# A two-layer RWKV-7 and attention trunk: the norm factor moved into the inverse blocks, and recurrence steps moved between ScalarE, VectorE and GpSimd

## The chip, the cores and the metric

One core of one Trainium2 chip runs the whole program in one launch. The metric is the device time in microseconds. The engines are PE (TensorE), DVE (VectorE), ACT (ScalarE), POOL (GpSimd) and SP (SyncE, which here only issues DMA transfers; POOL and ACT issue some too).

## The reference

The input x has 1024 tokens of 1024 features in float32. Layer 0 is RWKV-7 time mixing and an MLP, layer 1 forgetting attention and an MLP. The change lies in the time mixing, whose core is, for each of 16 heads of 64 features:

```python
kk = kk / jnp.maximum(jnp.linalg.norm(kk, axis=-1, keepdims=True), 1e-12)
k = k * (1.0 + (a - 1.0) * k_a)
b_h = kk * a_h
def step(S, inp):
    r_t, w_t, k_t, v_t, kk_t, b_t = inp
    sa = jnp.einsum('bhvk,bhk->bhv', S, -kk_t)
    S = (S * w_t[:, :, None, :] + sa[..., None] * b_t[:, :, None, :]
         + v_t[..., None] * k_t[:, :, None, :])
    y_t = jnp.einsum('bhvk,bhk->bhv', S, r_t)
    return S, y_t
...
y = (y - mean) * lax.rsqrt(var + GN_EPS)
y = y * lnx_w + lnx_b
y = (y + bonus) * g
return y @ w_o
```

Before it stand the projections to r, k, v and the low-rank branches for the decay w, for a and for the gate g; after it the residual, and `square(relu(h @ w_in)) @ w_out`.

## The kernel before

The step by step recurrence is computed in 16 chunks of 64 tokens. Within a chunk the tokens' mutual effect is a triangular system, whose inverse is made ahead in blocks of 32 tokens (32x32), for all heads and chunks.

In order of time: the low-rank branches (to about 53 us); the k projection, whose results `prep_pair` turns, pair of heads by pair of heads (8 pairs), into decayed k, kk and b (written to DRAM as `d_KR`, `d_BK`), the blocks `d_N`, and the factor `nt`, one over the squared norm of kk for each token and head (to 203); the r projection (to 281), with the first half of the inverse (`prep_inverse`, b=0) on DVE beside it; the v projection (to 371), with the second half (b=1); the gate projections (`gp`, to about 404); the recurrence, some 15 us a chunk (to about 676); the rest of the trunk.

`prep_inverse` keeps 128 blocks of 32x32 in `Tb` for each of two halves g, solves them with 31 pairs of DVE steps, and writes them to `d_B` and, transposed by a DVE copy into `Nb`, to `d_T`. From there `rec_load_blocks` reads three tiles for a chunk: `B11` and `BT2` (for the corner that joins two blocks of 32) and `TT` (the whole 64x64 inverse, whose off-diagonal corner `rec_corner2` writes). Before, `nt` was not in the blocks but in a table `ns2`, and was multiplied into `B11` and into the solution `Z` of each chunk.

PE's order within chunk c: `pp` (Z by AE, the state's part), an early part of the output `yp` (KR by Z); then `ap` of chunk c+1 (b, k against kk, r), which DVE masks into `AE`; `sa` (the inverse `TT` by `Ps`, the copy of pp), which becomes half of `Z`; `tp` (transposes of b, k, copied to `BKt`); `u` (the new state, needs Z and BKt), the rest of `yp`, the corner products `op`. In chunks 3 and later 24 matmuls of the output projection `wo` are spread over a chunk. KR (kk and r with their decays; its tile and BK's are named KRz in the profile) lies in two buffers, one per parity of chunks. After `ap` of a chunk has read KR, r's half is scaled by the decay of the chunk before (`rec_corner`), for the next early output.

The matrix `w_o` is loaded in 8 parts (`woraw`), each split into a rounded high part on ACT (`woh`) and a low part `wol`. The table WO gives for each part the hook numbers at which its load, its high part and, if a third number is there, its low part on DVE are placed; without the third number the low part is a GpSimd step. ACT's casts `woh` are pinned: `keep_in_program_order` holds them in the order in which they are written among other pinned ACT steps. All other steps are ordered on each engine by a list scheduler with a timeline model; `high_priority(offset=900)` lifts the solve and the state.

The parts on which the prediction's steps rest are the loads in `rec_load`, the end of `rec_corner`, the end of `rec_solve`, and in `stage_recurrence` where the next chunk's loads are asked for:

```python
            prev, cur, Z = cur, nxt, Zn
            if c + 2 < NCH:
                nxt, Zn = load(c + 2)
```

Of the kernel before, what the change touches and what calls it, by code (L numbers as in the profile page):

```python
# [8 lines left out]
F32 = mybir.dt.float32  # L9
# [7 lines left out]
P = 128  # L17
# [12 lines left out]


XAT = (2, 4, 6, 8, 10, 12, 13, 14)
WO = {1: (0, 1), 2: (0, 3), 3: (3, 5), 0: (5, 11), 4: (9, 16, 21), 7: (12, 23, 28), 5: (14, 17), 6: (18, 24)}
# [124 lines left out]
def rwkv_keep(k):  # L158

    cp, dr = k.const, k.dram  # L160

    k.sc = cp.tile([P, NK, NCH], F32, name="sc")
    k.ns2 = cp.tile([P, NK, NCH], F32, name="ns2")

    k.bon = cp.tile([P, NK, H], F32, name="bon")
    k.d_vb = dr.tile([2, T, NK, N], F32, name="d_vb")
    k.d_vh = dr.tile([2, T, NK, N], F32, name="d_vh")
    k.d_KR = dr.tile([NCH, P, NK, 2, C], F32, name="d_KR")
    k.d_BK = dr.tile([NCH, P, NK, 2, C], F32, name="d_BK")
# [33 lines left out]
def head_sums(k, xs, pool):  # L203
# [10 lines left out]
    for j in range(2):  # L214
        nc.tensor.transpose(bank[:, 256 + P * j:256 + P * j + P], rows[:, P * j:P * j + P], k.ident)
# [54 lines left out]
def prep_pair(k, p, units):  # L270

    nc, w = k.nc, k.pw
    nt = w.tile([P, HC, 2], F32, tag="nt", name="nt")
    nc.vector.tensor_scalar(nt.rearrange("p (g j) h -> p g j h", j=2), head_sums(k, [u[0] for u in units], w), 1e-24, -1.0,
                            op0=ALU.max, op1=ALU.mult)
    nc.vector.reciprocal(nt, nt)
    np_ = [k.psA.tile([P, HC, C], F32, tag="psA", name="np_") for _ in HALF]
    for c in range(NCH):
        for h, hs in enumerate(HALF):
            _, KK, BK = units[c // HC]  # L280
            nc.tensor.matmul(np_[h][HALF[c % 2], c // 2], BK[hs, c % HC, 0], KK[hs, c % HC], start=True, stop=True)
    for h in range(2):
        N_ = units[h][1]
        nc.vector.tensor_tensor(N_, np_[h], nt[:, :, h:h + 1].broadcast_to([P, HC, C]), op=ALU.mult)
        u = 2 * (p % 4) + h
        for c in range(2):
            for d in range(2):
                s0 = u % 4 * 32 + (c * 2 + d) * HC
                q = 64 * c + 32 * d
                nc.sync.dma_start(k.d_N[p // 4][u // 4, s0:s0 + HC].rearrange("c i t -> i c t"),  # L290
                                  N_[q:q + 32, :, 32 * d:32 * d + 32])
# [26 lines left out]
def prep_inverse(k, b, pool):  # L318

    nc = k.nc  # L320
    Nb, Tb = (k.pi.tile([P, 2, 32, 32], F32, tag=n, name=n) for n in ("Nb", "Tb"))
    Tm = pool.tile([P, 512], F32, tag="v", name="Tm", bufs=3)
    nc.gpsimd.dma_start(Nb, k.d_N[b].rearrange("g s i t -> s g i t"))
    ones = Tb.rearrange("p g t m -> p g (t m)")
    nc.gpsimd.memset(ones, 0.0)
    nc.gpsimd.memset(ones[:, :, 0:1024:33], 1.0)
    for j in range(31):
        n, m = 31 - j, j + 1
        S = [P, 2, n, m]
# [70 lines left out]
    return Z  # L400


def rec_load(k, c):

    nc, w = k.nc, k.rw
    (KR, BK), TT = k.KRB[c % 2], k.TT[c % 2]
    B11 = k.rc.tile([P, NK, 32], F32, tag="B11", name="B11")
    BT2 = k.rc.tile([P, NK // 2, 32], F32, tag="BT2", name="BT2")
    nc.sync.dma_start(KR, k.d_KR[c])
    nc.sync.dma_start(BK, k.d_BK[c])  # L410
    AE = w.tile([P, NK, 2, 2, C], F32, tag="AE", name="AE")
    BKt = w.tile([P, NK, P], F32, tag="BKt", name="BKt")
    return dict(c=c, KR=KR, TT=TT, BK=BK, B11=B11, BT2=BT2, AE=AE, BKt=BKt)


def rec_load_blocks(k, s):

    nc, c, TT, B11, BT2 = k.nc, *(s[n] for n in ("c", "TT", "B11", "BT2"))
    dT = k.d_T.rearrange("(p r) m t -> r m p t", r=64)
    dB = k.d_B.rearrange("(p r) t m -> r t p m", r=64)  # L420
    r0, r1 = ([32 * h + (2 * (c % 2) + d) * HC + c // 2 for h in range(2)] for d in range(2))
    for h in range(2):
        nc.sync.dma_start(B11[QUART[h]], dB[r0[h]])
# [29 lines left out]
def rec_corner(k, s):  # L453

    nc, c = k.nc, s["c"]
    AE, KR = s["AE"], s["KR"]
    O1 = s["O1"] = k.rw1.tile([P, NK // 2, 32], F32, tag="O1", name="O1")
    op = k.psA.tile([P, NK // 2, 32], F32, tag="psA", name="op")
    for p in range(NK):
        for h, q in enumerate(QUART):  # L460
            k.pe.matmul(op[LANES[h][p % 2], p // 2], AE[q, p, h, 0, 32:64], s["B11"][q, p], start=True, stop=True)
    nc.scalar.copy(O1, op)
    if c:

# [17 lines left out]
def rec_solve(k, s, Z):  # L482

    nc, c = k.nc, s["c"]
    pp = k.psC.tile([P, NK, C], F32, tag="psC", name="pp")
    for p in range(NK):
        for h, hs in enumerate(HALF):
            k.pe.matmul(pp[hs, p], s["AE"][:, p, h, 0, :], Z[:, h, p], start=True, stop=True)
    Ps = k.rw.tile([P, NK, C], F32, tag="Ps", name="Ps")
    if c:  # L490
        nc.scalar.copy(Ps, pp)
    else:
        nc.vector.tensor_copy(Ps, pp)
    yp = s["yp"] = k.psY.tile([P, NK, C], F32, tag="psY", name="yp")
    if c:
        for p in range(NK):
            for h, hs in enumerate(HALF):
                k.pe.matmul(yp[hs, p], s["KR"][hs, p, 1, :], Z[hs, h, p], start=p == 0, stop=False)
    yield
    sa = k.psC.tile([P, NK, C], F32, tag="psC", name="sa")  # L500
    for p in range(NK):
        for h, hs in enumerate(HALF):
            k.pe.matmul(sa[hs, p], s["TT"][:, p, h, :], Ps[:, p], start=True, stop=True)
    for h, hs in enumerate(HALF):
        nc.vector.tensor_tensor(Z[hs, h], sa[hs], k.ns2[hs, :, c:c + 1].broadcast_to([64, NK, C]), op=ALU.mult)
# [30 lines left out]
def rec_norm(k, s):  # L536
# [21 lines left out]
    eng.tensor_tensor(Y, Y, V, op=ALU.add)  # L558
# [1728 lines left out]
```

## Time and profile before

| | |
|---|---|
| median of 3 runs (lowest, highest) | 2512.4 us (2508.08, 2515.24) |
| the profiled execution, its span | 2515.11 us, 2513.4 us |
| mean granted clock of PE | 0.995 |
| busy: PE, DVE, ACT, POOL | 2471.0, 1820.6, 1288.0, 457.0 us |
| HBM | 166 GB/s over the span |

Times in the trace are microseconds from the span's start. A timeline row gives start, length, engine, line, operation, the written tile <- the read ones, shapes, and in brackets the idle time before it with what ended it. A row of waits gives a waiting engine's operation, the releasing one, and the sum, number and longest of the waits. A window of the trace gives each engine's busy time in it, then PE's granted clock, the share of the DMA engines and GB/s.

### The profile page before, as it was taken

The page shows a single profiled execution, that of the slowest core. Times are in us where ns is not written, and L with a number is a line of the kernel's source. Part 1 is how long each engine was busy: PE and PEld are TensorE (multiplying, and loading weights), DVE is VectorE, ACT ScalarE, POOL GpSimd, SP SyncE. Part 2 cuts the span into 40 slices and gives each one's busy share as a digit, 9 for nine tenths or more (in the row PEclk, how much of TensorE's full clock was granted, in tenths as well). Part 3 has the DMA queues.
Part 4 walks back from the last instruction along what each step waited for, and adds up shares of the span by engine and source line. Part 5 has one row for each costly group of instructions (what it writes and reads, how often), then busy time and mean ns, then how long its engine had stood idle before and what let it go on. Part 6 is the DMA issues. An engine that isn't in the chain of part 4 may idle for free.

```text
span 2513.4 us, 43433 instructions
## 1 busy us (share of the span) xinstructions
PE 2471.0 (98%) x16945; PEld 2062.8 (82%) x16945; DVE 1820.6 (72%) x2861; ACT 1288.0 (51%) x2236; POOL 457.0 (18%) x397
## 2 busy tenths in 40 slices
PE   8999998899999999999999999999999999999999
PEld 5777787788888888888889999888888888878887
DVE  7787995888687777477669576888528777656765
ACT  6782464333554555344456453788526455443332
POOL 2221135555200000003002223355100000000210
PEclk9999999999999999999999999999999999999999
DMA  4779668666244454766631325565323545386663
GB/s 140 168 159 225 176 221 221 182 178 172 78 161 150 150 169 167 264 247 238 220 113 51 118 76 169 146 151 144 130 82 120 169 150 171 117 287 236 224 209 135
DMA packets 378801, 419.79 MB, mean 167 GB/s; under 512 B 141786, under 2 KB 257970, under 8 KB 378596
## 3 DMA queue, kind: packets, MB, share of 16 engines
q1 hardware_dynamic: 366196, 389.88, 51.5%
q0 software_dynamic: 5744, 18.69, 2.0%
q10 hardware_dynamic: 6656, 8.46, 1.0%
q8 instruction: 133, 2.18, 0.4%
q14 instruction: 72, 0.59, 0.1%
HBM read 293.02 MB, written 123.92 MB: 166 GB/s over the span
## 4 chain that ended last, share of the span: by engine, by line
PE 90%; DVE 3%; issue 2%; DMA 2%; ACT 2%; POOL 1%; SPq 1%; ACTq 0%; DVEq 0%; POOLq 0%
PE mm L381 42%; PE mm L800 7%; PE mm L801 7%; PE mm L799 7%; PE mm L869 5%; PE tp L384 4%; PE wo L381 3%; PE mm L898 3%; PE s L381 2%; PE o L381 2%; PE z1p L381 1%; PE yp L381 1%; PE ap L381 1%; PE u L381 1%; PE sa L381 1%
## 5 line engine op out<-in xcount | busy, mean ns | idle before, releaser
L381 PE MATMUL mm<-ol,oh 128*128 128x512 f32 x896 | 346.8, 389 | 1.0 <-DVE ol L1614 1.0
L381 PE MATMUL mm<-oh 128*128 128x512 f32 x896 | 346.9, 389 | 0.4 <-ACT oh L1612 0.4
L381 PE MATMUL mm<-oh,ol 128*128 128x512 f32 x896 | 346.6, 389 | 0.0
L763 ACT CAST oh<-ra 128x1024 fp32r<-128x1024 f32 x108 | 113.8, 1054 | 333.3 <-PE mm L381 239.3
L766 DVE TENSOR_TENSOR ol<-ra,oh 128x1024 fp32r<-128x1024 f32 x108 | 137.8, 1276 | 146.9 <-ACT oh L763 146.8
L381 PEld LDWEIGHTS mm<-ol,oh 128*128 128x128 f32 x896 | 168.2, 188 | 36.1 <-DVE ol L1614 1.4
L381 PEld LDWEIGHTS mm<-oh 128*128 128x128 f32 x896 | 168.2, 188 | 35.6 <-ACT oh L1612 0.8
L381 PEld LDWEIGHTS mm<-oh,ol 128*128 128x128 f32 x896 | 168.2, 188 | 35.0
L799 PE MATMUL mm<-xhT,ah 128*128 128x512 f32 x448 | 174.3, 389 | 0.0
L800 PE MATMUL mm<-xlT,ah 128*128 128x512 f32 x448 | 174.3, 389 | 0.0
L801 PE MATMUL mm<-xhT,al 128*128 128x512 f32 x448 | 174.3, 389 | 0.0
L1673 POOL DMA_DIRECT2D xt<-d_xh x8 | 4.4, 551 | 756.2 <-DMA rb<-in_mlp_w_out_dram 419.6
L763 ACT CAST ah<-w 128x512 fp32r<-128x512 f32 x128 | 79.3, 620 | 110.9 <-PE mm L800 99.5
L800 PE MATMUL mm<-xlB,ah 128*128 128x512 f32 x336 | 130.7, 389 | 0.0
L799 PE MATMUL mm<-xhB,ah 128*128 128x512 f32 x336 | 130.7, 389 | 0.0
L801 PE MATMUL mm<-xhB,al 128*128 128x512 f32 x336 | 130.7, 389 | 0.0
L766 DVE TENSOR_TENSOR ol<-rb,oh 128x1024 fp32r<-128x1024 f32 x92 | 120.7, 1312 | 0.3 <-ACT oh L763 0.3
L2005 ACT ACTIVATE l<-l,mx 128x512 f32<-128x512 f32 (+7 forms) x128 | 99.4, 778 | 26.7 <-DVE mx L2002 26.2
L1430 ACT ACTIVATE z<-z 128x512 f32<-128x512 f32 x112 | 70.8, 633 | 75.6 <-DVE z L1427 74.5
L799 PEld LDWEIGHTS mm<-xhT,ah 128*128 128x128 f32 x448 | 84.1, 188 | 17.6
L800 PEld LDWEIGHTS mm<-xlT,ah 128*128 128x128 f32 x448 | 84.1, 188 | 17.4
L801 PEld LDWEIGHTS mm<-xhT,al 128*128 128x128 f32 x448 | 84.1, 188 | 17.3
(516 smaller groups left out, 6655.3 us busy)
## 6 DMA issues: line engine op xcount, KB each, us to landing
rb<-in_mlp_w_out_dram SPq DMA_DIRECT2D x124, 512.0 KB, 5.6
ra<-d_H SPq DMA_DIRECT2D x108, 512.0 KB, 4.1
w<-in_mlp_w_in_dram SPq DMA_DIRECT2D x64, 512.0 KB, 4.3
d_H<-z SPq DMA_DIRECT2D x56, 512.0 KB, 3.8
d_H<-sums SPq DMA_DIRECT2D x32, 768.0 KB, 5.7
raw<-in_rwkv_w_rkv_dram SPq DMA_DIRECT2D x24, 512.0 KB, 5.0
KRz<-d_KR SPq DMA_DIRECT2D x16, 512.0 KB, 4.6
KRz<-d_BK SPq DMA_DIRECT2D x16, 512.0 KB, 5.2
```

The source lines that it names most:

```text
L381: return self.tc.keep_in_program_order(self.tc.nc.tensor.matmul(*args, **kw))
L384: return self.tc.keep_in_program_order(self.tc.nc.tensor.transpose(*args))
L763: nc.scalar.copy(hi, src)
L766: lo_eng.tensor_tensor(lo, src, hi.bitcast(F32), op=ALU.subtract)
L799: te.matmul(out, ah, bh, start=i == 0, stop=False)
L800: te.matmul(out, ah, bl, start=False, stop=False)
L801: te.matmul(out, al, bh, start=False, stop=i == n - 1)
L869: nc.tensor.matmul(o[e][half], wt[:, i % 4, es], xs[i][part][:, 512 * half:512 * half + 512], start=i == 0 and wt is hi and part == 0, sto ...
L898: nc.tensor.matmul(o, x[:, ts], y, start=i == 0 and m == 0, stop=i == NK - 1 and m == 2)
L1430: nc.scalar.activation(x, x if o is None else o, AF.Relu)
L1673: nc.gpsimd.dma_start(xt[i], k.d_xh[i * P:i * P + P, :])
L2005: nc.scalar.activation(l, l, AF.Exp, bias=m, scale=-1.0, accum_out=SM[:, j, qb:qb + 1])
```

## The change

It has six parts. (1) The table `ns2` goes, with its 32 copies and the multiplies into `B11` and `Z`; instead `nt` is transposed on PE for each pair, copied by ACT and written to a DRAM table `d_nt` (two transfers a pair), and `prep_inverse` reads it and multiplies `Tb` by it on GpSimd, one step of 128x1024 for each g, ahead of the writes of `d_B` and `d_T`. (2) r's scaling by the decays goes from two GpSimd steps a chunk to eight ACT steps of 128x64. (3) KR and BK of chunk c+2 are asked for in `rec_fetch`, right after the early output of chunk c, not at the chunk's end. (4) The low parts 4 and 7 of w_o go from DVE to GpSimd. (5) The first half of Z is now a copy on ACT and the second one on DVE (both on DVE in chunks 0 and 1), where both were DVE multiplies. (6) The last two steps of the output's norm (by `lnw`, plus `Vh`) go to GpSimd in chunks 0 to 2, as in the others before.

```diff
-WO = {..., 4: (9, 16, 21), 7: (12, 23, 28), ...}
+WO = {..., 4: (9, 16), 7: (12, 23), ...}
...
# setup
-    k.ns2 = cp.tile([P, NK, NCH], F32, name="ns2")
+    k.d_nt = dr.tile([2, 2, P, 32], F32, name="d_nt")
...
# prep_pair
-    beside(nc.gpsimd.tensor_copy, k.ns2[:, p], nt)
+    rows = k.psB.tile([P, 512], F32, tag="psB", name="nt_ps")
+    nc.tensor.transpose(rows[0:16, 0:P], nt.rearrange("p c h -> p (c h)"), k.ident)
+    row = w.tile([16, P], F32, tag="ntrow", name="ntrow")
+    nc.scalar.copy(row, rows[0:16, 0:P])
+    for h in range(2):
+        u = 2 * (p % 4) + h
+        nc.sync.dma_start(k.d_nt[p // 4, u // 4, 32 * (u % 4):32 * (u % 4) + 32].rearrange("(c d j) t -> j c d t", c=2, d=2),
+                          row[h::2].rearrange("j (c d t) -> j c d t", c=2, d=2))
...
# prep_inverse
+    nt = k.pi.tile([P, 2, 32], F32, tag="nti", name="nti")
+    nc.gpsimd.dma_start(nt, k.d_nt[b].rearrange("g s t -> s g t"))
     for g in range(2):
+        nc.gpsimd.tensor_tensor(Tb[:, g], Tb[:, g], nt[:, g].unsqueeze(2).broadcast_to([P, 32, 32]), op=ALU.mult)
         r0 = (2 * b + g) * P
         nc.gpsimd.dma_start(k.d_B[r0:r0 + P], Tb[:, g])
...
+def rec_fetch(k, c):
+    KR, BK = k.KRB[c % 2]
+    k.nc.sync.dma_start(KR, k.d_KR[c])
+    k.nc.sync.dma_start(BK, k.d_BK[c])
...
# rec_load
-    nc.sync.dma_start(KR, k.d_KR[c])
-    nc.sync.dma_start(BK, k.d_BK[c])
...
# rec_load_blocks
-    for q in QUART:
-        nc.gpsimd.tensor_tensor(B11[q], B11[q], k.ns2[q, :, c:c + 1].broadcast_to([32, NK, 32]), op=ALU.mult)
...
# rec_corner
-        for i, eng in enumerate((nc.vector, nc.gpsimd)):
-            for h, hs in enumerate(HALF):
-                sc = k.sc[hs, :, c - 1:c].broadcast_to([64, NK, C])
-                eng.tensor_tensor((AE[hs, :, h, 0], KR[hs, :, 1])[i], KR[hs, :, i], sc, op=ALU.mult)
+        for h, hs in enumerate(HALF):
+            sc = k.sc[hs, :, c - 1:c].broadcast_to([64, NK, C])
+            nc.vector.tensor_tensor(AE[hs, :, h, 0], KR[hs, :, 0], sc, op=ALU.mult)
+        for p in range(NK):
+            nc.scalar.mul(KR[:, p, 1], KR[:, p, 1], k.sc[:, p, c - 1:c])
...
# rec_solve
-        nc.vector.tensor_tensor(Z[hs, h], sa[hs], k.ns2[hs, :, c:c + 1].broadcast_to([64, NK, C]), op=ALU.mult)
+        (nc.vector.tensor_copy if h or c < 2 else nc.scalar.copy)(Z[hs, h], sa[hs])
...
# rec_norm
-    eng = nc.vector if c < 3 else nc.gpsimd
-    eng.tensor_tensor(Y, Y, k.lnw, op=ALU.mult)
-    eng.tensor_tensor(Y, Y, V, op=ALU.add)
+    nc.gpsimd.tensor_tensor(Y, Y, k.lnw, op=ALU.mult)
+    nc.gpsimd.tensor_tensor(Y, Y, V, op=ALU.add)
...
# stage_recurrence
+            rec_fetch(k, 0)
             cur = rec_load(k, 0)
...
+        rec_fetch(k, 1)
         nxt, Zn = load(1)
...
                 next(solve)
+            if c + 2 < NCH:
+                rec_fetch(k, c + 2)
```

How the order moves is shown at three places. The first is POOL, from the end of the gate inputs (`xt`) to the first low part. Before:

```order
L766 TENSOR_TENSOR xt_3597<-raw,xt_3596 128x4x128
L1239 TENSOR_TENSOR xt_3598<-raw,xt_3598 32x4x128
L357 MEMSET TT_3826 128x1024
L357 MEMSET TT_3829 128x1024
L361 MEMSET mask 128x512
L399 MEMSET Z 64x512 x2
L365 AFFINE_SELECT mask<-mask 64x4x64 x4
L432 TENSOR_TENSOR B_3843<-B_3843,ns_89 32x256 x2
```

After:

```order
L776 TENSOR_TENSOR xt_3621<-raw,xt_3620 128x4x128
L1249 TENSOR_TENSOR xt_3622<-raw,xt_3622 32x4x128
L337 TENSOR_TENSOR Tb<-Tb,nti 128x1024 x2
L339 DMA d_B<-Tb 128x1024
L341 DMA d_T<-Nb 128x1024
L339 DMA d_B<-Tb 128x1024
L341 DMA d_T<-Nb 128x1024
L360 MEMSET TT_3850 128x1024
L360 MEMSET TT_3853 128x1024
L364 MEMSET mask 128x512
L402 MEMSET Z 64x512 x2
L368 AFFINE_SELECT mask<-mask 64x4x64 x4
```

The second inverse's writes, which stood ahead of the `xt` steps, now follow them, behind the two new multiplies, and the fills of `TT`, `mask` and `Z` follow the writes.

The second place is the queue that SP issues, from the load of `lnw` to the first writes of the gates. Before:

```order
L1213 DMA woraw<-in_rwkv_w_o_dram 64x1024 x4
L371 DMA lnw<-in_rwkv_lnx_w_dram 64x8x64 x2
L397 DMA Z<-d_vh 64x512 x2
L423 DMA B_3843<-d_B 32x8x32 x2
L426 DMA BT_3844<-d_T 32x4x32 x4
L430 DMA TT_3826<-d_T 32x8x32 x4
```

After:

```order
L374 DMA lnw<-in_rwkv_lnx_w_dram 64x8x64 x2
L400 DMA Z<-d_vh 64x512 x2
L431 DMA B_3869<-d_B 32x8x32 x2
L1223 DMA woraw<-in_rwkv_w_o_dram 64x1024 x4
L434 DMA BT_3870<-d_T 32x4x32 x4
L438 DMA TT_3850<-d_T 32x8x32 x4
```

The first two parts of w_o move behind `lnw`, `Z` and the load of `B11` from `d_B`. They are loaded into memory that `prep_inverse` used.

In the same queue, further on, chunk 2's KR and BK. Before:

```order
L1213 DMA woraw<-in_rwkv_w_o_dram 64x1024 x2
L543 DMA Vh<-d_vb 64x512 x2
L565 DMA g<-d_g 128x8x128
L409 DMA KRz_3825<-d_KR 128x1024
L410 DMA KRz_3825<-d_BK 128x1024
```

After:

```order
L438 DMA TT_3853<-d_T 32x8x32 x4
L400 DMA Z<-d_vh 64x512 x2
L409 DMA KRz_3849<-d_KR 128x1024
L410 DMA KRz_3849<-d_BK 128x1024
L1223 DMA woraw<-in_rwkv_w_o_dram 64x1024 x2
L550 DMA Vh<-d_vb 64x512 x2
L571 DMA g<-d_g 128x8x128
```

The two loads go ahead of the loads of w_o, `Vh` and `g`.

The third place is ACT in a chunk of the steady part. Before:

```order
L550 ACTIVATE ysq<-Y 128x512
L577 CAST zh<-Y 128x8x64
L86 ACTIVATE rs_t<-var,eps_72 128x8
L88 ACTIVATE rsd<-rs_t 128x8
L479 COPY TT_3829<-op_5253 32x4x32 x4
L491 COPY Ps<-pp 128x512
L450 COPY BKt<-tp 128x512 x2
```

After:

```order
L557 ACTIVATE ysq<-Y 128x512
L583 CAST zh<-Y 128x8x64
L86 ACTIVATE rs_t<-var,eps_72 128x8
L88 ACTIVATE rsd<-rs_t 128x8
L486 COPY TT_3853<-op_5297 32x4x32 x4
L498 COPY Ps<-pp 128x512
L475 ACTIVATE KRz_3849<-KRz_3849,sc 128x64 x8
L512 COPY Z<-sa 64x512
L456 COPY BKt<-tp 128x512 x2
```

Nine instructions come in between `Ps` and `BKt`. In chunks 2 and 3 the casts `woh` stand there as well.

More of the change, by code (lines that the diff above doesn't have):

```diff
@@ L32 @@
 XAT = (2, 4, 6, 8, 10, 12, 13, 14)
-WO = {1: (0, 1), 2: (0, 3), 3: (3, 5), 0: (5, 11), 4: (9, 16, 21), 7: (12, 23, 28), 5: (14, 17), 6: (18, 24)}
+WO = {1: (0, 1), 2: (0, 3), 3: (3, 5), 0: (5, 11), 4: (9, 16), 7: (12, 23), 5: (14, 17), 6: (18, 24)}
 EARLY = [1, 2, 3]
@@ L216, in head_sums @@
     return bank[:, 256:512].rearrange("p (j g x) -> p g j x", j=2, g=4)[:, :, :, 0:2]
-def beside(copy, dst, sums):
-    for h, hs in enumerate(HALF):
-        for c in range(2):
-            copy(dst[hs, c::2], sums[HALF[c], :, h])
 def prep_decay(k, p, hf, lora):
@@ L463, in rec_corner @@
     if c:
-        for i, eng in enumerate((nc.vector, nc.gpsimd)):
-            for h, hs in enumerate(HALF):
-                sc = k.sc[hs, :, c - 1:c].broadcast_to([64, NK, C])
-                eng.tensor_tensor((AE[hs, :, h, 0], KR[hs, :, 1])[i], KR[hs, :, i], sc, op=ALU.mult)
+        for h, hs in enumerate(HALF):
[3 more added lines that the diff above has]
+            nc.scalar.mul(KR[:, p, 1], KR[:, p, 1], k.sc[:, p, c - 1:c])
 def rec_corner2(k, s):
```

## The prediction

> **What bounds the kernel now.** I read the page first, then windows of 20 us, the waits of PE, and the timelines of PE, DVE, ACT, POOL and the DMA queue where PE is not full.
>
> ```profile
> PE 2471.0 (98%) x16945; PEld 2062.8 (82%) x16945; DVE 1820.6 (72%) x2861; ACT 1288.0 (51%) x2236; POOL 457.0 (18%) x397
> 200.00:220.00 20.00, 17.16 (x73) 13.27 (x73) 11.19 (x23) 4.17 (x7) 0.00 (x0) 0.93 0.82 173
> 220.00:240.00 20.00, 20.00 (x84) 14.13 (x83) 19.62 (x31) 4.00 (x7) 0.00 (x0) 0.90 1.06 230
> 400.00:420.00 20.00, 17.05 (x381) 13.78 (x379) 10.74 (x18) 11.81 (x26) 10.82 (x8) 1.00 0.93 265
> 420.00:440.00 20.00, 15.97 (x300) 14.46 (x302) 14.87 (x20) 6.19 (x15) 7.91 (x7) 0.83 0.93 240
> 440.00:460.00 20.00, 16.30 (x320) 14.28 (x318) 16.76 (x28) 8.95 (x19) 9.79 (x9) 0.83 0.82 212
> 460.00:480.00 20.00, 16.29 (x272) 13.87 (x269) 16.92 (x26) 4.78 (x12) 11.78 (x10) 0.91 0.55 154
> 480.00:500.00 20.00, 20.00 (x400) 17.31 (x400) 16.19 (x27) 6.99 (x16) 10.74 (x11) 1.00 0.70 189
> ...
> PE u L381 <- DVE Z L505: 6.2, 7, 2.7
> PE ap L381 <- DMA KRz<-d_BK: 5.3, 1, 5.3
> PE sums L210 <- DVE kr L313: 2.8, 1, 2.8
> PE tp L384 <- DVE AE L442: 2.1, 2, 1.5
> PE yp L381 <- DVE Z L505: 1.2, 2, 0.8
> ```
>
> After its span and time, a window's columns are PE, PEld, DVE, ACT, POOL (busy, instructions), PE's granted clock, DMA share and GB/s. PE is busy for 2471.0 us, so a moved step can save only where PE waits or runs at a lower clock. From 480 on the recurrence (it starts at 404) gives PE no idle time and a clock of 1.00: whatever the change takes from POOL or DVE there is worth nothing. What can be won lies in chunks 0 to 3 (400 to 480: 14.4 us idle, clock 0.83 to 1.00) and at 215 (2.8 us).
>
> ```profile
> 423.70 3.78 PE L381 MATMUL ap<-KRz 64*128 64x128 f32 x32 [5.33 <-DMA KRz<-d_BK]
> 427.42 1.84 PE L381 MATMUL sa<-Ps,TT 128*64 128x64 f32 x32
> 446.59 0.48 PE L381 MATMUL u<-Z,BKt 128*64 128x64 f32 x2 [1.99 <-DVE Z L505]
> 447.31 1.86 PE L381 MATMUL u<-Z,BKt 128*64 128x64 f32 x29 [0.25 <-DVE Z L505]
> 465.61 0.33 PE L381 MATMUL u<-Z,BKt 128*64 128x64 f32 x2 [2.65 <-DVE Z L505]
> 467.86 2.01 PE L381 MATMUL yp<-Z,AE 128*64 128x64 f32 x31
> ...
> 553.87 2.06 PE L381 MATMUL ap<-KRz 64*128 64x128 f32 x32
> 555.86 1.15 PE L381 MATMUL sa<-Ps,TT 128*64 128x64 f32 x32
> 558.90 1.17 PE L381 MATMUL u<-Z,BKt 128*64 128x64 f32 x32
> ```
>
> The last three rows are a steady chunk. Against them, work after a wait is slower as well: ap 3.78 for 2.06, u 1.86 for 1.17.
>
> **The change part by part.**
>
> *b, k, r loaded earlier.* The page's largest single stall here is the 5.33 us before ap at 423.70, and the matmuls behind it lose 1.72 (ap) and 0.69 (sa): 7.7 us.
>
> ```profile
> 212.05 5.01 DMA kr<-d_BK
> 415.15 8.42 DMA KRz<-d_BK
> ```
>
> Both rows are of the chain of waits. A load beside the r projection takes 5.01 us to land; chunk 2's takes 8.42 from 415.15, beside a DMA share of 0.93. In the new order these two loads stand ahead of a w_o load (two DMAs), Vh's two and g's, where they were behind all five. The stall goes if they are ahead by 5.3 us. But the same bytes still cross the engines in 400 to 440 (0.93 of 40 us is 37 us of work), so other loads become later. I take -6, range 0 to -7.7. Next late there are TT and the values' Z.
>
> *Norm factor into the inverse blocks.* The 32 copies on POOL and the multiply before each Z disappear at nothing by themselves: in steady chunks PE is full. New are the following.
>
> ```profile
> 381.41 1.28 POOL L1239 TENSOR_TENSOR xt<-raw,xt 32x512 fp32r<-32x512 f32 x1
> 397.56 2.39 POOL L605 TENSOR_TENSOR wol<-woraw,woh 128x1024 fp32r<-128x1024 f32 x1 [6.60 <-issue]
> 379.42 2.44 SPq L1213 DMA_DIRECT2D woraw<-in_rwkv_w_o_dram  x4
> 396.36 1.07 ACT L600 CAST woh<-woraw 128x1024 fp32r<-128x1024 f32 x1
> 401.32 1.21 PE L381 MATMUL gp<-xt,xt 128*128 128x512 f32 x4 [0.25 <-ACT gs L1286]
> woraw<-in_rwkv_w_o_dram SPq DMA_DIRECT2D x14, 256.0 KB, 5.3
> ```
>
> (The last row is of the DMA issues, 377 to 440, median us to landing.) For the second inverse (b=1) the multiplies stand behind POOL's xt steps, which end at 382.7. Two of 128x1024 with two inputs, at 2.39 us each (w_o's low part, the same shape), end at 387.5; the TT fills and the mask come after them and d_B, d_T. SP issued the first w_o loads at 379.42; now they stand behind a load of B that waits for d_B, and their memory is free only when d_T has landed. With two POOL transfers to issue and land after 387.5 (the row nearest in kind, kr's, took 5.01), they start at about 395 and land at 395 + 5.3, some 400 to 402. ACT casts the first at 396.36 with no wait, in a fixed place ahead of the gate copies, and gate matmuls wait for those copies (401.32). So ACT stands 4 to 6 us, PE up to that, less what it can do without them. I take +4, range 0 to +8.
>
> ```profile
> 153.28 0.38 PE L215 MATMUL sums<-ident,hrows 128*128 128x128 f32 x2
> 206.12 4.18 SPq L290 DMA_DIRECT2D d_N<-KK  x8
> 211.40 1.28 SPq L302 DMA_DIRECT2D kr<-d_BK  x2
> 219.08 3.71 PE mm L869 x8
> 229.20 4.56 PE mm L869 x20
> ```
>
> In the k stage PE gets a transpose per pair of heads: 8 at 0.38/2 = 0.19 us is +1.5 (range +1 to +2), on the path, since PE is the bound there. The 16 d_nt transfers are issued by SP, at about 0.5 us each (4.18/8); the last four fall after 200 and stand ahead of kr's load, whose issue at 211.40 and landing (5.01) set the 2.8 us wait of sums and the slow matmuls after it (3.71 for 8, where one takes 4.56/20 = 0.23: 1.9 lost). That makes kr 2 us later. Against it, sums stands 14 matmuls later in PE's new order (3.2 us at 0.23). Of the 2.8 + 1.9 I take -1, range -5 to +3. The first inverse's multiplies lie under the r projection.
>
> *r's decays on ScalarE; S copied by two engines; Y and w_o's low parts on GpSimd.*
>
> ```profile
> 317.95 1.77 ACT L1083 ACTIVATE vb<-tv,bon 128x64 f32<-128x64 f32 x7
> 558.54 0.59 ACT L450 COPY BKt<-tp 128x512 f32<-128x512 f32 x1 [0.32 <-PE tp L384]
> 443.80 0.94 DVE L558 TENSOR_TENSOR Y<-Y,Vh 128x512 f32<-128x512 f32 x1
> 460.83 2.38 POOL L605 TENSOR_TENSOR wol<-woraw,woh 128x1024 fp32r<-128x1024 f32 x1
> 461.39 2.37 DVE L558 TENSOR_TENSOR Y<-Y,Vh 128x512 f32<-128x512 f32 x1
> ```
>
> Eight 128x64 multiplies on ACT are 8 x 0.25 = 2.0 us a chunk (1.77/7). In a steady chunk each follows its own ap matmul (from 553.87), so they run from about 554.2 to 556.2; sa ends at 557.0; Z's half (0.59, as a copy of BKt) ends at 557.6, and BKt's second copy stays at 558.54, where it waits for PE. Twelve chunks: 0.
>
> Chunk 2 (u at 446.59): DVE loses L558's 0.94 from between its AE steps (tp waits for AE twice, 2.1 in all) and half of Z; but ACT now has a cast (1.07), 2.0 of multiplies and a second cast (1.07) ahead of its half of Z and of BKt, so u starts some 0.8 sooner and gets back part of its 0.7 of clock: -1.5, range 0 to -4. Chunk 3 (u at 465.61): L558's 2.37 goes, and ACT has one cast only. That is most of the 2.65, and u's and yp's clock (yp 2.01 for about 1.15): -4, range -2 to -5. At the end yp waits 0.8 less for Z: -0.8 (0 to -0.8).
>
> The L558 row beside POOL's 460.83 row shows what sharing costs: 2.37 us against 0.94, done only when POOL is. The change gives POOL two more low parts and six more Y steps, and takes from it the multiplies on B and r.
>
> The Trainium skill ("SBUF — State Buffer", section "SBUF: two separate sides") says that a GpSimd step that reads SBUF and a VectorE step with two SBUF inputs hold a shared port pair one at a time, the other waiting for the whole step. By that rule, which the 2.37 bears out, the two added low parts could each hold a DVE step for up to 2.4 us in chunks 1 and 2, and the sum would be some 4.8 less of a gain; I leave it out of the sum, since DVE's steps on the path there (AE, Z) take an input from PSUM.
>
> **Sum**: +4 - 6 + 1.5 - 1 - 1.5 - 4 - 0.8 = -7.8, on the profiled execution's 2515.1: 2507.3. That execution lies 2.7 above the median of the three runs, 2512.4, so the median comes to 2504.6, 0.31% less. Runs of this kernel lie within 0.3% (7.5 us), which is my bound for "same".
>
> **The rivals.**
> - *The gate stage eats it.* If w_o's first load waits for d_T as long as its upper end says, PE loses 8 instead of 4, and loads that come due in the same stretch leave half of the -6: -0.8 in all, 2511. For it: SP's order, and DMA at 0.93. Against: PE may have other gate and chunk-0 work in the gap.
> - *All waits go.* Entry 0, load -7.7, chunks 2 and 3 -4 and -5, r stage -5: with +1.5 and -0.8 that is -21; two thirds of it -15, 2497. For it: each is a wait with one named cause; against: DMA at 0.93 and ACT's longer queue.
> - *Slower: ACT becomes the bound of a chunk.* Z's half has to start by 558.54 - 2 x 0.59 = 557.4, so the multiplies may take (557.4 - 554.2)/8 = 0.40 us each. At 0.6 they end at 559.0, u is 1.6 late in 12 chunks: +19 with the gains off, 2524. Against: 0.25 in the only row of that form, though with a PSUM-fresh input and no matmul between.
> - *The load isn't earlier.* SP comes to it as late as before because the loads of B, BT and Z ahead of it wait: -6 becomes 0, 2510.
> - *GpSimd holds DVE*: the 4.8 above, 2509.
>
> **How the numbers follow.** The forecast's own case (2500 to 2508) 0.45, gate stage 0.24, all waits 0.17, ACT bound 0.06, load no earlier 0.04, GpSimd 0.04. Faster means below 2504.9: of the first case, spread evenly, (2504.9 - 2500)/8 = 0.61 of 0.45, 0.28, and the second rival's 0.17: 0.45. Slower means above 2519.9: 0.06, and 0.02 of the gate stage's beyond its end: 0.08. The rest, 0.47, is same. The range 2494 to 2514 leaves out the ACT case (0.06) and some 0.12 at the ends of the two larger rivals.
>
> **What would show it.** Right: ap of chunk 2 with a wait under 2 us; w_o's first load issued after 390 and a new ACT wait for it, 3 to 6 us, near 396; L558 no more on DVE; Z <- sa on ACT and DVE side by side, 480 to 660 with PE full. Wrong: the ap wait still over 4 us; a wait of u for ACT's BKt or Z in chunks after 4 (the slower case); a new wait for TT or Vh's loads of the same size as the old; a gate stage with no loss, which would add 4 to the gain.

## The result: 0.7% slower, and the profile after

| | before | after |
|---|---|---|
| median of 6 runs each (lowest, highest) | 2509.13 us (2507.57, 2515.24) | 2528.30 us (2523.64, 2532.84) |
| after / before, 95% interval | | 1.0071 (1.0056, 1.0086) |
| profiled execution, its span | 2515.11, 2513.4 | 2526.92, 2525.2 |

The change costs 19.2 us by the medians; 2504.6 with a range of 2494 to 2514 had been predicted. The two profiled executions differ by 11.8 us only: before's lies 6.0 above its median, after's 1.4 below. The traces below therefore explain 11.8 us, and the timed runs decide the size. Of the kernels further down, two executions of e11 (2954 and 4820 us, at clocks of 0.78 and 0.94) ran in a slow state and are left out of its numbers.

The page of after, the busy time of the engines:

```profile
PE 2473.2 (98%) x16953; PEld 2062.7 (82%) x16953; DVE 1802.1 (71%) x2839; ACT 1327.5 (53%) x2378; POOL 404.5 (16%) x317
```

PE's busy time is nearly the same (2471.0 before), so nearly all of the loss is idle time. Windows of after, columns as before, with one more for the end of the v projection and the gate stage (371 to 404):

```profile
200.00:220.00 20.00, 20.00 (x129) 16.37 (x122) 3.25 (x6) 4.36 (x8) 0.00 (x0) 1.00 0.72 172
220.00:240.00 20.00, 19.24 (x92) 14.14 (x92) 18.78 (x35) 3.90 (x7) 0.00 (x0) 1.00 1.14 224
371.00:404.00 33.00, 22.09 (x95) 14.07 (x94) 30.96 (x38) 15.43 (x23) 16.13 (x14) 0.84 0.58 192
400.00:420.00 20.00, 18.44 (x200) 13.68 (x200) 8.88 (x12) 13.80 (x28) 12.00 (x14) 1.00 0.81 238
420.00:440.00 20.00, 17.38 (x328) 14.86 (x327) 13.07 (x22) 12.46 (x32) 8.66 (x5) 0.83 0.90 237
440.00:460.00 20.00, 14.50 (x282) 12.45 (x280) 12.10 (x21) 9.82 (x26) 8.88 (x7) 0.91 0.93 220
460.00:480.00 20.00, 18.66 (x378) 16.43 (x379) 14.00 (x23) 10.15 (x28) 12.71 (x10) 0.83 0.85 219
480.00:500.00 20.00, 20.00 (x316) 16.89 (x314) 15.74 (x27) 8.71 (x24) 5.56 (x5) 1.00 0.82 228
```

The 33 us of the gate stage in before:

```profile
371.00:404.00 33.00, 32.75 (x198) 23.46 (x199) 16.84 (x24) 19.25 (x34) 20.27 (x17) 1.00 0.68 180
```

Two rows of after stand out. In 200 to 220 DVE works 3.25 us, where it worked 11.19. In 371 to 404 PE loses 10.9 us, which it did not lose before, and DVE, busy for half of it before (16.84), is nearly full (30.96). PE's granted clock there is 0.84, for 1.00 before, so the matmuls after its waits run slower as well. What PE waited for in after, 371 to 500 (sum, times, longest):

```profile
PE mm L384 <- DVE lo L776: 6.7, 2, 6.0
PE mm L384 <- ACT hi L773: 4.1, 1, 4.1
PE u L384 <- ACT Z L512: 3.2, 1, 3.2
...
PE ap L384 <- DMA KRz<-d_BK: 0.4, 1, 0.4
```

The first two are new: 10.8 us of waiting for the split inputs of the gate projections (`lo` on DVE, `hi` on ACT). The wait of `ap` that the change was to remove is gone (0.4 for 5.3). Why DVE is late is seen in timelines. Before, the first and the last step of the inverse:

```profile
202.91 0.23 DVE L331 TENSOR_TENSOR Tm<-Nb,Tb 128x62 f32<-128x62 f32 x1 [2.14 <-DMA d_N<-KK]
...
344.89 0.22 DVE L331 TENSOR_TENSOR Tm<-Nb,Tb 128x62 f32<-128x62 f32 x1
```

After, the first step of each half, the last one, and what stands around them on DVE and PE:

```profile
220.57 0.69 DVE L312 TENSOR_TENSOR Er<-r,Er 128x512 f32<-128x512 f32 x1 [12.30 <-DMA Er<-d_E]
221.18 0.22 DVE L331 TENSOR_TENSOR Tm<-Nb,Tb 128x62 f32<-128x62 f32 x1
...
319.36 0.42 DVE L331 TENSOR_TENSOR Tm<-Nb,Tb 128x62 f32<-128x62 f32 x1 [8.39 <-DMA Nb<-d_N]
381.81 0.80 PE L384 MATMUL mm<-hi,whi 128*128 128x512 f32 x1 [4.13 <-ACT hi L773]
387.81 1.21 DVE L776 TENSOR_TENSOR lo<-t,hi 128x1024 fp32r<-128x1024 f32 x1
389.07 1.22 PE L384 MATMUL mm<-lo,whi 128*128 128x512 f32 x2 [6.04 <-DVE lo L776]
392.96 0.22 DVE L331 TENSOR_TENSOR Tm<-Nb,Tb 128x62 f32<-128x62 f32 x1
```

DVE stands 12.30 us for the load of r's decays, with the inverse queued behind that step, and starts the first half 18.3 us later than before. (Before, it stood 5.86 us for the same load, but with seven `Tm` of the inverse done.) The second half starts 28 us later, at 319.36 for 291.64, and runs to 393.4, into the gate stage, where it shares DVE with the gates' inputs; before it ended at 345.4.

### The profile page after: what moved, and what is told of

The parts are those of the page before. It is cut to its first block, busy times and chain, and to the rows that moved or that the text cites. A ratio compares the mean times of both kernels' runs of the same rounds, so it can differ in the third digit from the quotient of the medians.

```text
span 2525.2 us, 43536 instructions
## 1 busy us (share of the span) xinstructions
PE 2473.2 (98%) x16953; PEld 2062.7 (82%) x16953; DVE 1802.1 (71%) x2839; ACT 1327.5 (53%) x2378; POOL 404.5 (16%) x317
## 4 chain that ended last, share of the span: by engine, by line
PE 81%; DVE 5%; DMA 2%; issue 2%; SPq 1%; ACT 1%; POOL 0%; DVEq 0%; ACTq 0%; POOLq 0%
PE mm L384 41%; PE mm L809 7%; PE mm L810 7%; PE mm L811 7%; PE wo L384 3%; PE tp L387 3%; PE mm L879 2%; PE s L384 2%; PE o L384 2%; PE yp L384 1%; PE ap L384 1%; DVE Tm L331 1%; DMA woraw<-in_rwkv_w_o_dram 1%; DVE l L2012 1%; PE mm L908 1%
```

## The cause in DVE's order

Part 1 of the change adds no instruction to DVE at this place, and the diff moves none there. Yet DVE's order is another one. Before, around the inverse's first steps:

```
L284 TENSOR_TENSOR KK<-np__2014,nt 128x512
L331 TENSOR_TENSOR Tm<-Nb,Tb 128x62
L333 TENSOR_TENSOR Tb<-Tb,Tm 128x2x31
L331 TENSOR_TENSOR Tm<-Nb,Tb 128x120
L333 TENSOR_TENSOR Tb<-Tb,Tm 128x2x30x2
```

After:

```
L776 TENSOR_TENSOR wlo<-raw,whi 128x1024
L312 TENSOR_TENSOR Er<-r,Er 128x8x64
L331 TENSOR_TENSOR Tm<-Nb,Tb 128x62
L333 TENSOR_TENSOR Tb<-Tb,Tm 128x2x31
L331 TENSOR_TENSOR Tm<-Nb,Tb 128x120
L313 SCALAR_TENSOR_TENSOR kr<-Er,cols_416,kr 128x512
L333 TENSOR_TENSOR Tb<-Tb,Tm 128x2x30x2
L312 TENSOR_TENSOR Er<-r,Er 128x8x64
```

r's steps (`Er`, `kr`) now stand ahead of the inverse and between its steps; before, the first `Er` followed the seventh `Tm`. The experiments were to find which part does this, and whether the time follows from it.

## The experiments

Each kernel was timed in five rounds. The table gives its time over that of before with the 95% interval, the median of its runs and, from its one profiled execution, how much later or earlier than in before's trace it reached four places: the first bonus step of the v projection (`vb`, 317.7 in before), the first gate matmul (`gp`, 390.9), the state matmul of chunk 0 (`pp`, 404.35) and of chunk 4 (475.80); then the span (2513.4). Before was timed again beside each group, with medians of 2513.1 (e1 to e4), 2512.9 (e5 to e8) and 2513.2 (e9 to e12), 4 us above the 2509.1 that belong to after: so compare kernels by their ratios, not by their medians.

| kernel | ratio | us | vb | gp | pp 0 | pp 4 | span |
|---|---|---|---|---|---|---|---|
| after | 1.0071 (1.0056, 1.0086) | 2528.3 | -1.4 | +11.8 | +13.6 | +9.6 | +11.8 |
| e1: after without part 1 | 0.9992 (0.9983, 1.0002) | 2510.7 | -4.5 | -4.4 | -4.5 | -7.7 | -7.8 |
| e2: part 1 alone | 1.0112 (1.0097, 1.0127) | 2537.8 | -3.2 | +11.5 | +13.0 | +21.5 | +21.9 |
| e3: after, nti elsewhere | 0.9998 (0.9989, 1.0008) | 2511.7 | +6.9 | +6.5 | +6.6 | -0.6 | -0.7 |
| e4: after, first Er behind the inverse's 7th step | 1.0067 (1.0053, 1.0081) | 2528.8 | +3.7 | +14.0 | +16.1 | +12.3 | +14.1 |
| e5: e3, d_nt written by ACT's queue | 0.9966 (0.9952, 0.9980) | 2505.7 | -3.9 | -4.4 | -4.4 | -15.5 | -15.8 |
| e6: e1 without part 3 | 0.9997 (0.9986, 1.0009) | 2511.7 | -4.0 | -4.0 | -3.7 | -7.8 | -4.5 |
| e7: e1 without part 2 | 0.9994 (0.9982, 1.0007) | 2511.8 | -6.8 | -6.8 | -6.8 | -11.1 | -7.6 |
| e8: e1 without parts 4 and 6 | 0.9983 (0.9969, 0.9997) | 2507.7 | -3.9 | -3.9 | -4.0 | -9.8 | -8.8 |
| e9: before with an unused tile of 256 bytes | 1.0069 (1.0057, 1.0082) | 2530.6 | -2.1 | +10.1 | +10.3 | +14.0 | +17.9 |
| e10: after, d_nt written by ACT's queue | 1.0047 (1.0033, 1.0061) | 2524.1 | -2.7 | +8.6 | +10.6 | +8.0 | +7.6 |
| e11: e5 without part 3 | 0.9981 (0.9969, 0.9992) | 2506.9 | 0.0 | -0.6 | -0.6 | -5.7 | -5.5 |
| e12: e5 without parts 4 and 6 | 0.9988 (0.9980, 0.9996) | 2510.3 | -1.3 | -1.8 | -1.8 | -4.7 | -2.7 |

One profile differs from the next by some us where nothing was changed: the -4 at `vb` stands in e1 too, which changes nothing up to there. In before's trace the windows 200 to 240 show clocks of 0.93 and 0.90, where after and e5 have 1.00 in both. Differences between columns of one row are safer than a row's offset; e5's profiled execution (2499.4) is 6.4 us faster than its median.

The times of e5, e9, e10 and e12 came as their main theory had them. e1, e2 and e3 came 2 to 6 us slower than theory A's ranges, which had counted from before's 2509; e4 fell into rival B's range, which e3 and e9 then exclude; e7 and e8 lay between their two cases. In e6 and e11 the wait of `ap` came back, but the times are those of the case in which it does not matter.

**e1 and e2: which part.** e1 keeps the table `ns2` with its multiplies (so part 5 falls as well: both halves of Z are DVE multiplies); e2 is before with part 1 alone.

```diff
# e1, against after (e2 does the opposite to before)
+    beside(nc.gpsimd.tensor_copy, k.ns2[:, p], nt)
...
-    nt = k.pi.tile([P, 2, 32], F32, tag="nti", name="nti")
-        nc.gpsimd.tensor_tensor(Tb[:, g], Tb[:, g], nt[:, g].unsqueeze(2).broadcast_to([P, 32, 32]), op=ALU.mult)
...
```

> The changed kernel with part 1 undone: the factor is in the table ns2 again and is multiplied into B11 and Z; parts 2 to 6 stay, except that both halves of Z are again DVE multiplies. Theory A (the loss comes from part 1: the second inverse ends late because the first one is queued late on DVE): 2500 to 2507 us, as the recurrence alone gained 4 us between its first pp and the last chunk with a wait. Rival C (the loss comes from the moved steps of parts 2 to 6): 2520 or more.

> The kernel before with part 1 alone. Theory A: 2522 to 2532 us (before 2509; the entry to the recurrence was 13.6 us later in the changed kernel, and nothing of parts 2 to 6 gives some of it back). Rival C: 2507 to 2511.

The whole loss is part 1's: alone it costs 1.12%, without it the change is within 0.2% of before. From e2 to after the ratio falls by 0.41%, some 10 us: parts 2 to 6 are worth that much once part 1 is in. Without it they are worth some 2 us (0.08%, an interval of -0.02 to 0.17). The waits of PE in e1, 400 to 480, point to a reason:

```profile
PE op L381 <- POOL B L437: 4.7, 2, 3.0
...
PE zp L384 <- POOL Y L563: 3.4, 1, 3.4
```

With the multiplies on B still there, GpSimd has these, the two low parts and the Y steps in chunks 0 to 2, and PE waits 8.1 us for it.

**e3, e4 and e9: what in part 1.** In e3 the tile `nti` (256 bytes a partition) comes from the pool of constants `cp`, and the rest is after. In e4 r's first `Er` is put behind the seventh multiply of the first inverse. e9 is before, with a tile of the same size in the pool of the inverse (`pi`), which GpSimd fills with zeros and nothing reads.

```diff
# e3
+    k.nti = cp.tile([P, 2, 32], F32, name="nti")
...
-    nt = k.pi.tile([P, 2, 32], F32, tag="nti", name="nti")
+    nt = k.nti
...
# e4 (k.inv_lead is the multiply of step 6 in the first half)
-                    kr.append(receptance(...))
+                    with nullcontext() if e else tc.issue_after(k.inv_lead.ins):
+                        kr.append(receptance(...))
...
# e9, in before's prep_inverse
+    pad = k.pi.tile([P, 2, 32], F32, tag="pad", name="pad")
+    nc.gpsimd.memset(pad, 0.0)
```

> The changed kernel, all six parts; only the tile nti (256 bytes of each partition) is taken from the pool of constants instead of the pool pi that holds Nb and Tb. All work, transfers and engines are the same; the order on DVE puts the first inverse ahead of r's Er step again. Theory A (order, by the memory that the pool's tiles reuse): second inverse ends near 350 instead of 393, 2503 to 2510 us. Rival B (the work of part 1 itself: 16 transfers more on SP, two multiplies on POOL ahead of d_B and of w_o's first load): still 2523 to 2532.

> The changed kernel; r's first Er step on DVE is queued behind the multiply of the seventh step of the first inverse, nothing else. Theory A in its narrow form (the loss is DVE's 12.3 us of idle time ahead of Er): the first inverse ends 12 us earlier, 2512 to 2519 us. Theory A in its wide form (the inverse also stands behind more of the v and gate inputs in DVE's order): 2518 to 2526. Rival B: 2526 to 2530.

> The kernel before, with nothing of the change; only prep_inverse takes one more tile of 256 bytes of each partition from the pool pi, which GpSimd fills with zeros behind the inverse and nobody reads. Theory A (the second inverse is late because the added tile shifts what memory the pool's tiles reuse, and with it DVE's order): first inverse behind r's Er on DVE, second inverse ending after 380, PE waiting for the gate inputs, 2520 to 2532 us. Rival B (the work of part 1 is the cause): 2507 to 2514, as before.

e9 decides: an unused tile costs 0.69%, the whole change 0.71%. In its order DVE has `wlo`, `Er`, `Tm` of 62, `Tb`, `Tm` of 120, `kr`, as after has and before has not. Its timeline on DVE, and what PE waited for in 371 to 500:

```profile
211.73 0.69 DVE L312 TENSOR_TENSOR Er<-r,Er 128x512 f32<-128x512 f32 x1 [8.79 <-DMA Er<-d_E]
212.34 0.22 DVE L331 TENSOR_TENSOR Tm<-Nb,Tb 128x62 f32<-128x62 f32 x1
...
375.50 0.23 DVE L331 TENSOR_TENSOR Tm<-Nb,Tb 128x62 f32<-128x62 f32 x1
```

```profile
PE ap L383 <- DMA KRz<-d_BK: 7.6, 1, 7.6
PE mm L383 <- DVE lo L768: 7.5, 3, 5.3
...
PE mm L383 <- ACT hi L765: 4.0, 1, 4.0
```

The same kind of stall ahead of the first inverse, a late end of the second one (its last multiply at 375.50, for 344.89 in before), and the same two waits in the gate stage (11.5 us; 10.8 in after), with none of the change's work: the two fills of the tile take 0.19 us each. The other way round, e3 takes the tile out of that pool: the inverse starts at 207.33, its last multiply at 353.20, no wait for `lo` or `hi` is left, and 0.73% of the time comes back. So the loss comes from where 256 bytes lie, in a pool that takes memory which earlier stages have used, and the traces show its way: DVE's order, the late inverse, PE's wait in the gate stage. Which earlier tile's memory it is, and by what rule the order turns on it, was not found. One candidate stands in the code and was not tested: `pi` and the pool of r's loads (`Er`, `kr`) are opened one behind the other when an earlier pool closes, with waits for each reused tile (`reuse_waits="tile"`), so one more tile in `pi` may shift all that follows onto the memory of other tiles. The rest of the change comes out even (e3 0.9998): what it gains, other costs take.

e4 shows that the stall of 12.30 us is not the cause by itself. There the first inverse starts at 207.0, as in e3, but the later steps are still spread among other work: the second half runs from 321.7 to 394.2, `lo` costs PE 7.6 us, and the time stays at 1.0067. This fits the whole order counting, and not its first row alone.

**e5 and e10: a second cost of part 1.** In e3 PE still reaches `vb` 6.9 us later than in before. The 16 transfers to `d_nt` go to ACT's queue in e5 (from e3) and e10 (from after):

```diff
-        nc.sync.dma_start(k.d_nt[...
+        nc.scalar.dma_start(k.d_nt[...
```

> E3's kernel (all six parts, nti in the pool of constants) with the 16 d_nt transfers issued by ACT instead of SP. Theory D (what part 1 still costs in E3, 6.5 us at the entry to the recurrence, comes from SP: r's first Er load is issued at 218.3 there, at 210.9 before, and PE waits 6.4 us for kr): Er's load before 214, the wait of sums for kr 3 us or less, 2504 to 2508 us. Rival (the transposes and the later end of the k stage on PE, not SP): 2510 to 2513, as E3.

> The changed kernel with the d_nt transfers issued by ACT, nti still in the pool pi. Theory A: DVE's order is still the late one, so this gains nothing or a little: 2518 to 2529 us. If SP's queue were the main cause of the loss: 2505 to 2513.

e3, the issue of r's first load of decays on SP, and PE's first step that needs r's product:

```profile
218.32 0.48 SPq L300 DMA_DIRECT2D Er<-d_E  x1
...
226.54 1.07 PE L211 MATMUL sums<-kr,heads 128*32 128x256 f32 x4 [6.42 <-DVE kr L314]
```

The same in e5:

```profile
213.06 0.45 SPq L300 DMA_DIRECT2D Er<-d_E  x1
...
219.37 0.62 PE L211 MATMUL sums<-kr,heads 128*32 128x256 f32 x4 [2.96 <-DVE kr L314]
```

In before that load was issued at 210.90. SP comes to it 7.4 us later in e3, with the writes of `d_nt` in front of it, and with the 16 on ACT's queue 5.3 of these come back. The move is worth 0.32% from e3 to e5; from after to e10 it is 0.24%, with intervals that overlap.

A third cost stays. In the k stage PE waits for ACT's copy of the head sums (`sums` <- `hrows`): 3.8 us in after, 3.2 to 5.0 in every kernel with part 1, and 1.2 in every one without it (before, e1, e6 to e9). In e5 it is 3.2, where e3 has 4.9. What in part 1 brings it was not taken apart.

e5 is the best version: 0.34% (0.20 to 0.48) faster than before, 1.0% than after. Its window 404 to 480, in which before's chunks 0 to 3 lie:

```profile
404.00:480.00 76.00, 67.36 (x1398) 57.69 (x1396) 57.46 (x98) 43.19 (x118) 36.88 (x26) 1.00 0.88 235
```

PE's clock is 1.00 in it, where before's four windows had 1.00, 0.83, 0.83 and 0.91.

**e6, e7, e8, e11 and e12: the other parts.** Each is undone by itself, in e1 and, for two, in e5.

```diff
# e6, e11: KR and BK of chunk c+2 again at the chunk's end
-            if c + 2 < NCH:
-                rec_fetch(k, c + 2)
...
             if c + 2 < NCH:
+                rec_fetch(k, c + 2)
                 nxt, Zn = load(c + 2)
# e7: r's decays on GpSimd again
+        for i, eng in enumerate((nc.vector, nc.gpsimd)):
...
-        for p in range(NK):
-            nc.scalar.mul(KR[:, p, 1], KR[:, p, 1], k.sc[:, p, c - 1:c])
# e8, e12: low parts 4 and 7 and the Y steps of chunks 0 to 2 on DVE again
-WO = {..., 4: (9, 16), 7: (12, 23), ...}
+WO = {..., 4: (9, 16, 21), 7: (12, 23, 28), ...}
...
+    eng = nc.vector if c < 3 else nc.gpsimd
...
```

> E1's kernel (parts 2 to 6) with part 3 undone: KR and BK of chunk c+2 are asked for at the end of chunk c again. If part 3 is worth what its wait was (5.3 us and the slow matmuls behind it): ap waits 4 to 6 us again for KRz in chunk 1, 2515 to 2519 us. If the loads only change places, and another one is late instead: 2510 to 2512.

> E1's kernel with part 2 undone: r's decays on GpSimd again, two steps of 1.1 us a chunk, behind the B steps, w_o's low parts and Y in POOL's queue. If POOL's queue sets the pace in chunk 1 (op waits 4.7 us for POOL's B, zp 3.4 for POOL's Y in E1): 1 to 4 us more, 2512 to 2515. If ACT's queue does: 0 to 2 less.

> E1's kernel with parts 4 and 6 undone: w_o's low parts 4 and 7 and the Y steps of chunks 0 to 2 on DVE again. If POOL's queue sets the pace: the waits of op for B and of zp for Y (8.1 us together) fall under 2 us, 2503 to 2507. If DVE does: waits of u and tp for DVE of 5 us or more take their place, 2509 to 2513.

> E5's kernel with part 3 undone (KR and BK asked for at the chunk's end). In E5 PE goes from the first pp to the steady part at full clock, 11 us shorter than before. If the early load is needed for that: a wait of ap for KRz of 3 to 6 us in chunk 1 and half clock behind it, 2510 to 2514 us. If it only trades places with B's load, as with E1's kernel: 2504 to 2508.

> E5's kernel with parts 4 and 6 undone (w_o's low parts 4 and 7, and Y of chunks 0 to 2, on DVE). POOL has no steps on B there, so nothing of PE waits for POOL in E5, and DVE has room to lose: waits of u and tp for DVE come back, 2508 to 2513 us. If GpSimd's steps hold DVE's (the shared port), undoing them gains instead: 2500 to 2504.

In e1's setting none of the three shows a gain: e6 and e7 cannot be told from e1 (ratios 0.9992, 0.9997, 0.9994, with intervals of about 0.001 to each side), though `ap` waits 3.7 us again in e6; and e8, where GpSimd is relieved, is better by 0.09%, which the intervals do not settle. In e5's setting the earlier load gives 0.15% by the ratios (its undoing brings the wait back) and the steps on GpSimd 0.22%. The waits of PE, 400 to 480, in e11 and then in e12:

```profile
PE ap L385 <- DMA KRz<-d_BK: 7.1, 1, 7.1
```

```profile
PE tp L388 <- DVE AE L449: 5.7, 3, 2.4
PE u L385 <- DVE Z L513: 4.3, 5, 1.7
```

The same parts, 4 with 6, look harmful in e1 and useful in e5. The waits fit this: in e1 PE waits for GpSimd, which still has the multiplies on B, in e12 for DVE. By the times alone it is not settled: e8's interval overlaps e1's, e12's touches e5's (0.9980), and e11's overlaps it (0.9969 to 0.9992 against 0.9952 to 0.9980).

## Why the prediction was wrong, step by step

**The step that failed: the gate stage's entry.** +4 with bounds of 0 and +8 was given; chunk 0 starts 13.6 us later. The sum went wrong where it said that "the multiplies stand behind POOL's xt steps, which end at 382.7". That took for granted that the second inverse was over by then, as in before's trace (345). The same step in after, with SP's issue and ACT's cast behind it:

```profile
393.58 3.98 POOL L337 TENSOR_TENSOR Tb<-Tb,nti 128x1024 f32<-128x1024 f32 x2 [8.95 <-issue]
...
406.13 2.39 SPq L1223 DMA_DIRECT2D woraw<-in_rwkv_w_o_dram  x4
...
410.95 1.05 ACT L607 CAST woh<-woraw 128x1024 fp32r<-128x1024 f32 x1 [1.26 <-DMA woraw<-in_rwkv_w_o_dram]
```

The multiplies begin at 393.58, when the last inverse step is done, and not at 382.7; w_o's load is issued at 406.13 and not about 395; each follows the other by about what was reckoned (12.5 us here, 12.3 there). But the wait it was reckoned for, ACT's for w_o, is 1.26 us and not the 4 to 6 of the sum, since PE had been held by `lo` and `hi` for 10.8 us already. The price was put on the wrong wait, because the order was read on POOL, SP and ACT, which the diff names, and not on DVE, where the inverse stands. The rival "the gate stage eats it" named the right stage, with a mechanism and a price (2511) that were not the ones. Without the tile's effect the forecast would have missed too: e3, the same six parts, comes out even with before (0.9998) and not 0.31% faster. That e5's 0.34% is near the forecast is luck, as e5 is another kernel, with two of part 1's costs taken out of it.

**The recurrence.** The three terms there, -6, -1.5 and -4, make -11.5 from chunk 0 to chunk 4. That stretch took 71.45 us in before, 67.39 in after (-4.06), 64.30 in e3 (-7.15) and 60.34 in e5 (-11.11). So the total was reached in e5 alone; e3, with the same six parts and no wait for `lo` or `hi` either, falls short of it by 4.4, and `op` waits 4.9 us there for the load of B. The load's -6 can be read by itself: without it (e11) the stretch takes 66.38 us, 6.04 more than in e5. The steps moved to GpSimd weigh more than was thought: without them (e12) it takes 68.57, 8.23 more. From `pp` to `pp`, e5's chunk 1 (the earlier load) gains 3.6 us, chunk 2 4.7 and chunk 3 3.0. The gate matmuls still to be done in these chunks differ between the kernels (the last at 454.3 in before, 441.7 in e5, 468.3 in after), so a chunk's gain is not one part's alone. The `ap` of chunk 2 in after, which runs in chunk 1, and the `u` of chunk 1 behind it; then `u` of chunk 2, where ACT stands for w_o and PE for ACT:

```profile
436.46 2.06 PE L384 MATMUL ap<-KRz 64*128 64x128 f32 x32 [0.39 <-DMA KRz<-d_BK]
...
441.48 1.09 PE L384 MATMUL u<-Z,BKt 128*64 128x64 f32 x29 [0.40 <-DVE Z L512]
...
456.06 1.05 ACT L607 CAST woh<-woraw 128x1024 fp32r<-128x1024 f32 x1 [4.53 <-DMA woraw<-in_rwkv_w_o_dram]
457.01 2.01 ACT L475 ACTIVATE KRz<-KRz,sc 128x64 f32<-128x64 f32 x8
458.93 1.03 ACT L607 CAST woh<-woraw 128x1024 fp32r<-128x1024 f32 x1
459.86 0.57 ACT L512 COPY Z<-sa 64x512 f32<-64x512 f32 x1
460.49 0.47 PE L384 MATMUL u<-Z,BKt 128*64 128x64 f32 x2 [3.21 <-ACT Z L512]
461.29 1.86 PE L384 MATMUL u<-Z,BKt 128*64 128x64 f32 x29 [0.32 <-DVE Z L512]
```

`ap` waits 0.39 us and is as fast as in a steady chunk: that step was right. The eight multiplies take 2.01 us, as estimated from the row of `vb`. But the casts and multiplies ahead of Z's half, put at a gain of 1.5 in all, hold it until 459.86, because the first cast waits 4.53 us for its load: `u` waits 3.21, more than before's 1.99.

**The rest.** The transposes: 8 of 0.27 us are 2.2 us, for 1.5 (bounds 1 and 2). PE's longer wait for `hrows` (3.8 for 1.2) stood at nothing in the sum. The r stage, -1 (bounds -5 and +3): SP's delay of kr was put at 2 us, and the loads of r's decays, which stand beside it, are issued 5.1 us later in after than in before and 7.4 later in e3. With the transposes, the k and r stages were to come out at +0.5; measured against e1, which changes nothing in them, `vb` comes 3.0 us later in after, 11.3 in e3 and 0.6 in e5. After looks less harmed than e3 because DVE serves r ahead of the inverse there: PE's wait for `kr` is 0.8 us in after, 6.4 in e3, 2.8 in before. The steady part: PE was full in it again, and the twelve chunks cost nothing. The tail, -0.8, did not come: at the end `yp` waits 1.1 us for Z in after (0.7 for ACT, 0.4 for DVE), for 1.2 before. From chunk 4 to the end after loses 2.2 us against before and e5 gains 0.3. The 2.2 go with none of the parts: PE waits that long in the second layer (`s` for `mx` on DVE) in after, e4, e6, e7, e9 and e12, and not in before, e1, e2, e3, e5 or e10.

**The rivals.** ACT as the bound of every chunk did not come: its multiplies took 0.25 us each, not the 0.6 of that case. "The load isn't earlier" did not either. That GpSimd holds DVE, or DVE GpSimd, is seen in after where DVE's late steps meet POOL's four `xt` steps (377.34 to 384.64). Rows of DVE and POOL there; the forms of `t` and `vb` stand again further down, alone:

```profile
378.12 2.29 DVE L1015 SCALAR_TENSOR_TENSOR t<-hT,c_mug,t 128x1024 f32<-128x1024 f32 x1
379.41 2.13 POOL L1249 TENSOR_TENSOR xt<-raw,xt 32x512 fp32r<-32x512 f32 x1
380.34 1.75 DVE L1096 TENSOR_TENSOR vb<-vb,lnb 128x512 f32<-128x512 f32 x1
382.01 1.50 DVE L333 TENSOR_TENSOR Tb<-Tb,Tm 128x270 f32<-128x270 f32 x1
383.44 1.74 DVE L1096 TENSOR_TENSOR vb<-vb,lnb 128x512 f32<-128x512 f32 x1
385.11 1.27 DVE L1015 SCALAR_TENSOR_TENSOR t<-hT,c_mug,t 128x1024 f32<-128x1024 f32 x1
...
390.98 0.68 DVE L1096 TENSOR_TENSOR vb<-vb,lnb 128x512 f32<-128x512 f32 x1
```

Each of the DVE steps beside POOL is longer by 1.02 to 1.07 us (the `Tb` of 128x270 took 0.44 alone, in before at 207.21), and POOL's `xt` of 32x512 takes 2.13, where before's row at 381.41 has 1.28. So the collision adds some 4 us to DVE in the stage that was already late. It was not forecast there, and it is not the rival's case, which set the moved low parts against chunks 1 and 2: with those on GpSimd, e5 is 0.22% faster than e12 by the ratios, whose intervals touch. The Trainium skill ("SBUF — State Buffer", section "SBUF: two separate sides") has a shared port pair that a VectorE step with two SBUF inputs and a GpSimd step that reads SBUF hold in turn; these rows agree with it.

Two slips in the rivals' sums change nothing: two thirds of 21 are 14 and not 15, and 2512.4 less 0.8 is 2511.6.

## What to carry to other kernels

Where a scheduler orders the instructions and pools reuse memory, compare the new order with the old on every engine that feeds a wait, above all on those which the diff does not touch; a small tile in a pool that reuses memory can move work by tens of us. A control that adds the tile and none of the work found this in one run, and taking the tile from the pool of constants cured it here. Small transfers cost the queue that issues them: put new ones on a queue where what stands behind them is less urgent.

## What was not expected of the hardware

- In after PE's granted clock falls to half in 430 to 436, and `pp` takes 1.94 us for 30 matmuls (32 took 1.15 at 417.97):

```profile
430.00:436.00 6.00, 5.79 (x99) 4.69 (x97) 2.69 (x8) 3.86 (x11) 0.00 (x0) 0.50 0.97 282
432.23 1.94 PE L384 MATMUL pp<-Z,AE 128*64 128x64 f32 x30 [0.20 <-DMA Z<-d_vh]
```

  PE's longest waits between 418 and 430 were of 0.42 and 1.06 us (`op` for the load of B, at 426.59 and 427.86). `u` of chunk 2 ran at the same half pace after its wait of 3.21 us (1.86 us for 29, where chunk 1 took 1.09 after a wait of 0.40), and in before after a wait of 1.99 us with one of 1.46 a little ahead of it. The Trainium skill ("TensorE: Matmul & The Clock Gate", "Part 1: The HAM clock gate (the "warmup" mystery)") puts the drop behind at least one idle window of about 3.4 us; the rows here show it after waits that are shorter one by one. So waits of 1 to 2 us close to each other can be dearer on PE than their own length.
- The small writes take SP 0.7 to 0.8 us each to issue (`d_nt`, two in 1.43 to 1.66 us), and ACT's queue about as much in e5 (two in 1.63); there PE's wait for ACT's `hrows` was no longer than in e3 (3.2 us for 4.9).
